# One transformer step on one core: half of the cached attention moved beside an output projection, four adds of squares moved to VectorE

## The chip, the core and the metric

The kernel runs on one core of a Trainium2 chip. The time is the device time of one execution in microseconds (us): the median of three executions of the kernel before is 2620.69 us (2619.88 to 2621.56). A core has engines that run side by side, each in the order of its own instructions: TensorE (PE in the profile, with PEld for its loading of weights), VectorE (DVE), ScalarE (ACT), GpSimd (POOL) and SyncE (SP), which here issues most of the transfers (DMA). An instruction waits on semaphores of the engines or transfers whose results it needs.

## The reference, cut to what matters

One layer of a streaming encoder, for 512 prompt frames and for 8 sequences of 16 new frames each (640 columns in all). The input is normalised and projected, two groups of heads attend, each group's output is normalised by itself, and both together go through one output projection:

```python
def merge_and_ffn(x, oa, ob, norm_grp_a, norm_grp_b, w_out, norm_ffn, w_gate, w_up, w_down):
    o = jnp.concatenate([rmsnorm(oa, norm_grp_a), rmsnorm(ob, norm_grp_b)], axis=-1)
    x = x + o @ w_out
    h = rmsnorm(x, norm_ffn)
    return x + (jax.nn.silu(h @ w_gate) * (h @ w_up)) @ w_down
```

Group A is a chunk-band attention with 16 heads of 64; its 8 sequences also attend to 256 cached keys each ("decode" below). Group B is a grouped-query attention with a window and sinks. Each of oa and ob is 1024 features wide, that is 8 tiles of 128 features x 640 columns.

## The kernel before, in words

All is f32. A product is made of three matmuls on pairs of high and low parts (`mm3`, L207, L208, L209): the high part is a rounded copy (ScalarE, L198, or L202 with a gain), the low part the difference (VectorE, L199 or L203).

The program is emitted as dense matmuls with other work strewn in. The dense work (`dense`) multiplies weights by 640 columns: one k-step is two times three matmuls of 128x320, and after each k-step `tick` adds `rate` to a counter and calls `pump` once for each whole unit. `pump` takes turns over two streams, the prompt heads and decode, and advances one of them to its next `yield`. So `rate` is the pace of the side work against the dense work. `keep_pace` ties each PE instruction of side work behind the dense matmul emitted before it. `drain_queue` pumps until a queue is empty and the work taken from it has ended; `get` pumps where no tile is free. Results of dense work live in two PSUM tiles, named dn, those of side work in tiles named at. The tile names in rows below are the kernel's: S and W are slots of on-chip memory, sm is small numbers, x_d is a tensor in DRAM.

Around the change, in order:

- The input projections run with the heads and decode beside them. `decode_b` and `decode_a(0)` are queued at p == 4 with rate 1.1. `decode_a(g)` does the cached attention of half of group A (heads 8g to 8g + 7): it loads queries, keys and values (sa_d, L655), and then for each of 8 sequences loads cached keys (L677), copies columns (L674), makes scores (mm3 of 128x272), softmax (L697 to L707), loads cached values (L705), transposes the weights (L324), multiplies by the values (128x512), scales (L725), transposes again (L324) and puts the result in its columns (L734). At its end one store (L735) writes the four tiles' columns to oa_d.
- L830 drains decode, so that `decode_a(0)` ends before anything of group B's projection is emitted.
- `group_operands(o_d, gain, ssq, tiles)` loads each tile (L821), splits it with the gain (L202, L203) and adds its squares into the tile ssq (`add_square`: ScalarE squares at L280, the first directly into ssq at L277, and POOL adds at L281). It is called for group B's 8 tiles, then for group A's tiles 0 to 3 (at m == 11) and 4 to 7 (after the loop). All adds of one group go into one tile, one after another.
- `decode_a(1)` is queued.
- Group B's projection: 16 outputs m, each 8 k-steps on the 8 tiles. Behind the first, the sum of squares becomes the factor r_b (`rstd`: L251 sums over partitions, L253 to L258 make the inverse root, L263 spreads it, L268 copies it). Each result is multiplied by r_b (L843), added to x (L844) and stored to x2_d (L845).
- L850 drains all; A's tiles 4 to 7 are made, which need the store L735 of `decode_a(1)`.
- Group A's projection: the same with oa, whose results (L901) are added to what was stored (loads L900, add L902), squared and stored again (L905).

Of the kernel before, what the change touches and what calls it, by code (L numbers as in the profile page):

```python
# [45 lines left out]
def halves(ap):  # L46
    return ap.rearrange("p (a b) -> p a b", a=2)
# [255 lines left out]
def build(nc, tc, io, pools):  # L303
    n = Net(nc, tc, io, pools)
# [15 lines left out]
    def dram(name, shape):  # L320
        return pools["dr"].tile(list(shape), F32, tag=name, name=name)
# [11 lines left out]
    def pair(lst, k=TOK):  # L333
        a, b = n.get(lst), n.get(lst)
        return (a, b), (r(a[:, :k]), r(b[:, :k]))
# [481 lines left out]
    def group_operands(o_d, gain, ssq, tiles):  # L817
        own, out = [], []
        for t in tiles:
            o = n.get("S")  # L820
            dma(out=o, in_=o_d[t])  # L821
            two, hl = pair("S")
            n.split_gain(o, gain[:, t:t + 1], *hl)
            n.add_square(ssq, o, t == 0, "S")
            n.put("S", o)
            own.extend(two)
            out.append(hl)
        return own, out

    n.drain_queue("decode")  # L830
    r_b, ssq = n.get("S"), n.get("S")
    own_b, acts_b = group_operands(ob_d, g_b, ssq, range(8))
    n.add("decode", decode_a(1))
    x2_d, act_d = dram("x2_d", (KT, P, TOK)), dram("act_d", (7, P, NPAIR, 2, HT))
    first_d = dram("first_d", (7, P, 3, HT))
    r_a, ssq_a = n.get("S"), n.get("S")
    for m in range(KT):
        ps = n.dense([(io["w_out_b"][m], 8)], acts_b)
        if m == 0:
            n.rstd(ssq, 1024, r_b)  # L840
        xr, x = n.get("S"), n.get("S")
        dma(out=xr, in_=io["xT"][:, m])
        nc.vector.tensor_tensor(halves(x), ps, halves(r_b), ALU.mult)  # L843
        nc.vector.tensor_tensor(x, x, xr, ALU.add)  # L844
        dma(out=x2_d[m], in_=x)  # L845
        n.put("S", xr, x)
        if m == 11:
            n.drain_queue("heads")
            own_a, acts_a = group_operands(oa_d, g_a, ssq_a, range(4))
    n.drain()  # L850
    n.put("S", r_b, *own_b)
    n.move("D", "S", 10)


    more = group_operands(oa_d, g_a, ssq_a, range(4, 8))
    own_a, acts_a = own_a + more[0], acts_a + more[1]

# [320 lines left out]
    for t in range(STEPS - 2):  # L1178
        run(t)
        if t >= STEPS - 8:  # L1180
            if t == STEPS - 8:
                ssq = n.get("S")
# [143 lines left out]
```

## Time and profile before

| what | value |
|---|---|
| median of three executions | 2620.69 us (2619.88 to 2621.56) |
| the profiled execution | 2621.49 us, span 2619.7 us, mean granted clock of TensorE 0.997 |
| TensorE busy | 2565.2 us, 98% of the span, 17437 matmuls |
| VectorE busy | 2027.7 us, 77% |
| ScalarE busy | 1101.9 us, 42% |
| GpSimd busy | 663.8 us, 25% |
| mean transfer rate | 147 GB/s |

A row of the timeline has the start and duration in us, the engine, the line, the operation, what it writes and reads, the count, and in brackets how long the engine had idled ahead and on whom it waited. A row of the windows has the stretch, its length, the busy time of PE, PEld, VectorE, ScalarE and POOL with counts, the granted clock of TensorE (1.00 is full), the share of the transfer engines and GB/s. Matmuls overlap, so a matmul of 0.31 us may follow another after 0.15.

### The profile page before, as it was taken

How to read it: one execution, taken by the hardware profiler on the slowest of the kernel's cores; microseconds unless marked ns; L12 is line 12 of the kernel's file. 1: busy time of each engine (PE TensorE's matmuls, PEld its weight loads, DVE VectorE, ACT ScalarE, POOL GpSimd, SP SyncE). 2: the span in 40 equal slices, each digit the busy share in tenths (PEclk: the TensorE clock that was granted, in tenths of full speed). 3: DMA queues.
4: the chain of work that ended last, by engine and by line, in shares of the span. 5: the costliest groups of instructions: out<-in, count | busy, mean ns of one | idle time of the engine just before them, and what ended most of it. 6: DMA issues, size and time to landing. Idle time of an engine off the chain costs nothing.

```text
span 2619.7 us, 45100 instructions
## 1 busy us (share of the span) xinstructions
PE 2565.2 (98%) x17437; PEld 2527.9 (96%) x17437; DVE 2027.7 (77%) x3133; ACT 1101.9 (42%) x1797; POOL 663.8 (25%) x573
## 2 busy tenths in 40 slices
PE   8999999999999999999999999999999899999997
PEld 8999998999899999999999999999999899999996
DVE  5775676766866888788888888888888877777797
ACT  5553444444633644443433333433434333333343
POOL 0000000000301203332333333323324433333353
PEclk9999999999999999999999999999999999999998
DMA  5322232444655433443343343343445865666655
GB/s 172 101 69 91 94 102 86 133 124 130 214 188 185 155 131 122 160 162 126 131 142 126 130 144 123 131 146 120 133 147 176 280 189 157 175 175 169 192 156 176
DMA packets 178678, 383.87 MB, mean 147 GB/s; under 512 B 21856, under 2 KB 74080, under 8 KB 178464
## 3 DMA queue, kind: packets, MB, share of 16 engines
q1 hardware_dynamic: 154128, 326.92, 38.8%
q0 software_dynamic: 23184, 52.77, 7.1%
q8 instruction: 137, 2.24, 0.3%
q10 hardware_dynamic: 1152, 1.31, 0.1%
q14 instruction: 77, 0.63, 0.1%
HBM read 299.61 MB, written 80.58 MB: 145 GB/s over the span
## 4 chain that ended last, share of the span: by engine, by line
PE 85%; DVE 8%; DMA 3%; ACT 2%; issue 2%; POOL 0%; SPq 0%; DVEq 0%; ACTq 0%; POOLq 0%
PE dn L209 18%; PE dn L207 18%; PE dn L208 18%; PE at L207 9%; PE at L208 9%; PE at L209 9%; DVE W L199 2%; PE at L324 2%; DMA W<-w_down 1%; PE at L419 1%; DVE S L973 1%; ACT W L198 1%; PE at L215 1%; PE at L214 1%; ACT S L440 0%
## 5 line engine op out<-in xcount | busy, mean ns | idle before, releaser
L207 PE MATMUL dn<-S,W 128*128 128x320 f32 x3694 | 1152.5, 312 | 5.2 <-ACT S L1027 2.7
L209 PE MATMUL dn<-S,W 128*128 128x320 f32 x3694 | 1144.5, 310 | 6.7 <-DVE W L199 6.3
L208 PE MATMUL dn<-S,W 128*128 128x320 f32 x3694 | 1143.3, 310 | 2.0 <-DVE S L203 1.7
L198 ACT ACTIVATE W<-W 128x1024 fp32r<-128x1024 f32 (+2 forms) x632 | 608.2, 963 | 965.9 <-PE dn L208 542.8
L199 DVE TENSOR_TENSOR W<-W,W 128x1024 fp32r<-128x1024 f32 (+2 forms) x632 | 738.7, 1169 | 81.5 <-ACT W L198 77.6
L209 PEld LDWEIGHTS dn<-S,W 128*128 128x128 f32 x3694 | 694.1, 188 | 10.5 <-DVE W L199 10.1
L207 PEld LDWEIGHTS dn<-S,W 128*128 128x128 f32 x3694 | 694.7, 188 | 9.0 <-ACT S L1027 3.0
L208 PEld LDWEIGHTS dn<-S,W 128*128 128x128 f32 x3694 | 694.4, 188 | 4.1 <-DVE S L203 1.9
L209 PE MATMUL at<-S,W 128*128 128x320 f32 x1594 | 493.5, 310 | 4.9 <-DVE W L199 4.8
L207 PE MATMUL at<-S,W 128*128 128x320 f32 x1594 | 492.8, 309 | 0.5 <-ACT W L198 0.5
L208 PE MATMUL at<-S,W 128*128 128x320 f32 x1594 | 492.5, 309 | 0.0
L954 POOL TENSOR_TENSOR W<-W,W 128x1024 f32<-128x1024 f32 (+2 forms) x75 | 158.9, 2118 | 637.5 <-DVE W L199 453.6
L209 PEld LDWEIGHTS at<-S,W 128*128 128x128 f32 x1594 | 299.2, 188 | 7.3 <-DVE W L199 7.3
L207 PEld LDWEIGHTS at<-S,W 128*128 128x128 f32 x1594 | 299.3, 188 | 0.8 <-ACT W L198 0.8
L208 PEld LDWEIGHTS at<-S,W 128*128 128x128 f32 x1594 | 299.3, 188 | 0.0
L973 DVE TENSOR_TENSOR S<-S,dn 128x320 f32<-128x320 f32 x358 | 163.8, 480 | 65.4 <-PE dn L209 65.0
L963 POOL TENSOR_TENSOR W<-W,W 128x1024 f32<-128x1024 f32 (+2 forms) x75 | 163.6, 2181 | 118.9 <-DVE W L199 113.5
L949 DVE TENSOR_TENSOR W<-W,W 128x1024 f32<-128x1024 f32 (+2 forms) x76 | 124.6, 1640 | 62.8 <-DMA W<-w_down 29.5
L973 DVE TENSOR_TENSOR S<-S,at 128x320 f32<-128x320 f32 x262 | 123.3, 480 | 51.4 <-PE at L209 50.5
L980 POOL DMA_DIRECT2D S<-act_d x161 | 88.0, 547 | 178.6 <-PE dn L209 92.0
L951 DVE TENSOR_TENSOR W<-W,W 128x1024 f32<-128x1024 f32 (+2 forms) x76 | 83.4, 1097 | 61.6 <-DMA W<-w_up 31.4
L1044 DVE TENSOR_TENSOR S<-S,half 128x320 fp32r<-128x320 f32 x147 | 120.0, 837 | 1.9
(162 smaller groups left out, 2223.3 us busy)
## 6 DMA issues: line engine op xcount, KB each, us to landing
S<-act_d POOLq DMA_DIRECT2D x161, 320.0 KB, 3.7
W<-w_gate SPq DMA_DIRECT2D x88, 512.0 KB
W<-w_up SPq DMA_DIRECT2D x88, 512.0 KB
W<-w_in SPq DMA_DIRECT2D x66, 512.0 KB
W<-w_down SPq DMA_DIRECT2D x64, 384.0 KB
act_d<-half SPq DMA_DIRECT2D x147, 160.0 KB
act_d<-S SPq DMA_DIRECT2D x147, 160.0 KB
W<-w_down SPq DMA_DIRECT2D x68, 320.0 KB
```

Source lines behind the costliest of these rows:

```text
L198: self.nc.scalar.activation(hi, src, AF.Identity)
L199: self.nc.vector.tensor_tensor(lo, src, f(hi), ALU.subtract)
L207: mm(out, a[0], b[0], start=first, stop=False)
L208: mm(out, a[0], b[1], start=False, stop=False)
L209: mm(out, a[1], b[0], start=False, stop=last)
L949: nc.vector.tensor_tensor(b12[:, w], b12[:, w], b22[:, w], sub)
L951: nc.vector.tensor_tensor(s6[:, w], b11[:, w], b12[:, w], sub)
L954: eng.tensor_tensor(b11[:, w], b22[:, w], s6[:, w], sub)
L963: eng.tensor_tensor(b21[:, w], b21[:, w], s6[:, w], sub)
L973: add = lambda o, a, b: nc.vector.tensor_tensor(o, a, b, ALU.add)
L980: nc.gpsimd.dma_start(out=r(sh(t, 2, HT)), in_=r(act_d[which, :, j]))
L1044: nc.vector.tensor_tensor(r(src), src, hi, ALU.subtract)
```

## The change

The drain at L830 becomes a loop that pumps only until the decode queue is empty, that is, until `decode_a(0)` has been started. What is left of it goes on beside group B's projection, followed by `decode_a(1)`. At m == 11 the same loop makes sure that `decode_a(0)` has ended before A's tiles 0 to 3 are loaded. The rate is 1.22 after `decode_a(1)` is queued, instead of 1.1. In `group_operands`, the squares of tiles with an odd number are added by VectorE instead of POOL. That holds for all calls: tiles 1, 3, 5 and 7 of group B, and those of group A too, eight adds in all. Lines behind the change are two to four further down in the kernel after (L843 is L845, L844 is L846, L845 is L847, L900 is L904, L901 is L905, L905 is L909).

```diff
--- before.py
+++ after.py
@@ -821,16 +821,18 @@
             dma(out=o, in_=o_d[t])
             two, hl = pair("S")
             n.split_gain(o, gain[:, t:t + 1], *hl)
-            n.add_square(ssq, o, t == 0, "S")
+            n.add_square(ssq, o, t == 0, "S", nc.vector if t % 2 else None)
             n.put("S", o)
             own.extend(two)
             out.append(hl)
         return own, out
 
-    n.drain_queue("decode")
+    while n.queues["decode"]:
+        n.pump()
     r_b, ssq = n.get("S"), n.get("S")
     own_b, acts_b = group_operands(ob_d, g_b, ssq, range(8))
     n.add("decode", decode_a(1))
+    n.rate = 1.22
     x2_d, act_d = dram("x2_d", (KT, P, TOK)), dram("act_d", (7, P, NPAIR, 2, HT))
     first_d = dram("first_d", (7, P, 3, HT))
     r_a, ssq_a = n.get("S"), n.get("S")
@@ -846,6 +848,8 @@
         n.put("S", xr, x)
         if m == 11:
             n.drain_queue("heads")
+            while n.queues["decode"]:
+                n.pump()
             own_a, acts_a = group_operands(oa_d, g_a, ssq_a, range(4))
     n.drain()
     n.put("S", r_b, *own_b)
```

In the rows below, what follows the operation is what it writes and, behind the arrow, reads; in brackets stand the engines and transfer queues it waits for.

The first place is PE where the squares of group B are summed over partitions (L251; S_1305 after and S_1369 before is the sum of squares). Before:

```order
4418 L208 MATMUL dn_7978<-S_1383_7768,W_1440_7980 128x320
4419 L207 MATMUL at_7915<-S_1426_7916,S_1409_7836 128x272 [waits PE_49,DVE_49,Activation_49,Pool_49]
4420 L251 MATMUL at_7946<-gains,S_1369_7739 128x1 [waits PE_49]
4421 L251 MATMUL at_7946<-gains,S_1369_7739 128x1 x5
4422 L209 MATMUL dn_7978<-S_1382_7767,W_1441_7981 128x320
```
After:

```order
4352 L207 MATMUL dn_7754<-S_1314_7538,W_1376_7756 128x320
4353 L208 MATMUL dn_7754<-S_1315_7539,W_1376_7756 128x320
4354 L209 MATMUL dn_7754<-S_1314_7538,W_1377_7757 128x320
4355 L251 MATMUL at_7722<-gains,S_1305_7519 128x1 [waits DVE_49]
4356 L251 MATMUL at_7722<-gains,S_1305_7519 128x1 x5
4357 L207 MATMUL dn_7754<-S_1314_7538,W_1376_7756 128x320
```
Before, the sum stood in the first m behind a score product of decode and waited for nothing but PE's own work; now it stands 35 rows behind the transposes (L324) that close a sequence of decode, 27 of them dense, eight of L419, and waits for VectorE.

The second place is VectorE ahead of that, after the change: the adds of tiles 3, 5 and 7 into the sum, each waiting for POOL's add of tile 2, 4 or 6. L421 is a part of the prompt heads' softmax.

```order
1048 L281 TENSOR_TENSOR S_1305_7519<-S_1305_7519,S_1320_7551 128x640 [waits Pool_49]
1049 L421 ISA S_1347_7633,sm_7634<-at_7687,S_1343_7608 128x256 [waits PE_49]
1050 L421 ISA sm_7634 128x1
1051 L421 ISA S_1350_7636,sm_7637<-at_7688,S_1344_7609 128x256 [waits PE_49]
1052 L421 ISA sm_7637 128x1
1053 L281 TENSOR_TENSOR S_1305_7519<-S_1305_7519,S_1328_7569 128x640 [waits Pool_49]
1054 L421 ISA S_1346_7632,sm_7634<-at_7714,S_1343_7608 128x128 [waits PE_49]
1055 L421 ISA sm_7634 128x1
1056 L421 ISA S_1349_7635,sm_7637<-at_7715,S_1344_7609 128x128 [waits PE_49]
1057 L421 ISA sm_7637 128x1
1058 L281 TENSOR_TENSOR S_1305_7519<-S_1305_7519,S_1336_7587 128x640 [waits Pool_49]
```
Before, all seven adds stood on POOL and none of these rows had an add. L734 (two rows) and one L199 stand directly ahead of the first row.

The third place is the passage from group B to group A, where decode's last store (L735) and the loads of A's tiles 4 to 7 (L821) stand in SP's queue. Before:

```order
351 L735 DMA oa_d<-S_1407_7834 128x4x128 [waits DMAHW6_49,DVE_49]
352 L821 DMA S_1728_9573<-oa_d 128x640 [waits DMAHW7_49,DMAHW6_49]
353 L821 DMA S_1732_9582<-oa_d 128x640 [waits DMAHW0_49,Pool_49]
354 L821 DMA S_1736_9591<-oa_d 128x640 [waits DMAHW1_49]
355 L845 DMA x_d<-S_1715_9446 128x640 [waits DMAHW2_49,DVE_49]
356 L821 DMA S_1740_9600<-oa_d 128x640 [waits DMAHW3_49]
357 L219 DMA W_1757_9698<-w_out_a 128x1024 [waits DMAHW4_49,DVE_49]
358 L900 DMA S_1761_9753<-x_d 128x640 [waits DMAHW5_49,DMAHW2_49]
```
After:

```order
353 L847 DMA x_d<-S_1717_9484 128x640 [waits DMAHW0_49,DVE_49]
354 L904 DMA S_1755_9691<-x_d 128x640 [waits DMAHW1_49,PE_49]
355 L904 DMA S_1761_9753<-x_d 128x640 [waits DMAHW2_49,PE_49,Pool_49]
356 L904 DMA S_1777_9846<-x_d 128x640 [waits DMAHW3_49]
357 L735 DMA oa_d<-S_1431_8067 128x4x128 [waits DMAHW4_49,DVE_49]
358 L904 DMA S_1784_9910<-x_d 128x640 [waits DMAHW5_49,PE_49]
359 L821 DMA S_1728_9573<-oa_d 128x640 [waits DMAHW6_49,DMAHW4_49]
360 L821 DMA S_1732_9582<-oa_d 128x640 [waits DMAHW7_49,Pool_49]
```
The store now has three loads of x2_d (L904) directly ahead of it and a fourth between it and the loads of oa_d; before, these followed behind.

On PE at that passage, after the change, the fifth tile of A (S_1729 and S_1730) is used first in row 5364 by dn_9609 (A's first product), 49 rows behind the last transpose of decode (row 5315); before, there were 150 rows between (5209 and 5359).

```order
5360 L209 MATMUL dn_9697<-S_1635_9101,W_1759_9700 128x320 [waits DVE_49]
5361 L207 MATMUL dn_9697<-S_1635_9101,W_1758_9699 128x320
5362 L208 MATMUL dn_9697<-S_1636_9102,W_1758_9699 128x320
5363 L209 MATMUL dn_9697<-S_1635_9101,W_1759_9700 128x320
5364 L207 MATMUL dn_9609<-S_1729_9575,W_1746_9611 128x320 [waits Activation_49]
5365 L207 MATMUL dn_9697<-S_1638_9108,W_1758_9699 128x320
5366 L208 MATMUL dn_9697<-S_1639_9109,W_1758_9699 128x320
5367 L209 MATMUL dn_9697<-S_1638_9108,W_1759_9700 128x320
5368 L207 MATMUL dn_9697<-S_1638_9108,W_1758_9699 128x320
5369 L208 MATMUL dn_9697<-S_1639_9109,W_1758_9699 128x320
5370 L209 MATMUL dn_9697<-S_1638_9108,W_1759_9700 128x320
5371 L208 MATMUL dn_9609<-S_1730_9576,W_1746_9611 128x320 [waits DVE_49]
```
Rows of the second product (dn_9697) now stand between those of the first, and the last tile's low part (S_1742) is waited for in row 5400. Further down, the third product (dn_9790), which needs a PSUM tile that the first has left, now follows close behind L263, of which it needs the result:

```order
5428 L209 MATMUL dn_9697<-S_1741_9602,W_1759_9700 128x320
5429 L263 MATMUL at_9680<-cst,sm_9672 128x128 [waits DVE_49]
5430 L263 MATMUL at_9680<-cst,sm_9672 128x128
5431 L263 MATMUL at_9680<-cst,sm_9672 128x64
5432 L263 MATMUL at_9685<-cst,sm_9672 128x128 x2
5433 L263 MATMUL at_9685<-cst,sm_9672 128x64
5434 L207 MATMUL dn_9697<-S_1741_9602,W_1758_9699 128x320
5435 L208 MATMUL dn_9697<-S_1742_9603,W_1758_9699 128x320
5436 L209 MATMUL dn_9697<-S_1741_9602,W_1759_9700 128x320
5437 L207 MATMUL dn_9790<-S_1635_9101,W_1774_9792 128x320 [waits DVE_49,PE_49]
```
Before, 25 dense rows stood between L263 and the third product; now three do.

## The prediction

> **What bounds the kernel now.** The page comes first: engines, then the chain of waits.
>
> ```profile
> PE 2565.2 (98%) x17437; PEld 2527.9 (96%) x17437; DVE 2027.7 (77%) x3133; ACT 1101.9 (42%) x1797; POOL 663.8 (25%) x573
> PE 85%; DVE 8%; DMA 3%; ACT 2%; issue 2%; POOL 0%; SPq 0%; DVEq 0%; ACTq 0%; POOLq 0%
> ```
>
> TensorE (PE) is busy for 98% of the span. Its count of instructions is not touched by the change, so the change can only win or lose time in which PE stands still or runs at a lower clock. The busy time by stretches, over the decode tail, group B's projection (640 to 815) and one quiet stretch far behind, says how much of that there is. The columns are span, PE, PEld, DVE, ACT and POOL busy time, clock, DMA share and GB/s.
>
> ```profile
> 640.00:660.00 20.00, 18.92 (x122) 17.22 (x121) 14.17 (x30) 11.68 (x22) 2.18 (x4) 1.00 0.74 228
> 660.00:680.00 20.00, 17.58 (x120) 16.11 (x119) 19.74 (x51) 17.12 (x41) 11.14 (x10) 1.00 0.55 170
> 680.00:700.00 20.00, 17.18 (x108) 15.90 (x107) 15.47 (x37) 13.28 (x24) 5.12 (x12) 0.91 0.60 201
> 700.00:720.00 20.00, 19.94 (x132) 18.77 (x130) 12.84 (x29) 6.95 (x13) 2.77 (x10) 1.00 0.75 251
> 720.00:740.00 20.00, 19.65 (x135) 18.90 (x134) 12.86 (x28) 7.41 (x14) 2.13 (x6) 1.00 0.47 153
> 740.00:760.00 20.00, 19.74 (x131) 18.62 (x131) 13.21 (x33) 7.42 (x16) 1.00 (x5) 1.00 0.53 178
> 780.00:800.00 20.00, 18.41 (x124) 17.38 (x123) 14.39 (x27) 9.04 (x16) 6.42 (x6) 1.00 0.65 212
> 688.00:690.00 2.00, 2.00 (x11) 2.00 (x11) 2.00 (x4) 1.97 (x5) 0.61 (x1) 0.55 0.12 40
> 690.00:692.00 2.00, 2.00 (x11) 2.00 (x10) 1.50 (x11) 1.73 (x3) 0.00 (x0) 0.60 0.48 137
> 1000.00:1100.00 100.00, 100.00 (x684) 100.00 (x683) 80.46 (x92) 39.84 (x51) 32.93 (x17) 1.00 0.43 142
> ```
>
> In 640 to 700 PE idles 1.08 + 2.42 + 2.82 = 6.32 us; in 700 to 800 it idles 0.06 + 0.35 + 0.26 + 1.59 = 2.26 us. In 688 to 692 it works at clock 0.55 and 0.60, which costs 2 x 0.45 + 2 x 0.40 = 1.7 us. All that the change can win is therefore about **10.3 us**, 0.39% of the time. The last row gives the price of a dense matmul, 100 / 684 = 0.146 us.
>
> PE's waits between 480 and 900 name the releasers (us in total, times, longest):
>
> ```profile
> PE at L324 <- ACT S L699: 3.5, 6, 1.6
> PE dn L208 <- DVE S L203: 1.7, 1, 1.7
> PE at L324 <- DMA S<-sa_d: 1.5, 1, 1.5
> PE at L207 <- ACT S L198: 1.2, 2, 1.1
> PE at L207 <- DVE S L199: 0.7, 1, 0.7
> ```
>
> These are decode's short serial steps (softmax L699, splits L198 and L199, load of sa_d), unhidden because the drain emits them without dense matmuls around them, and one operand of group B (L203).
>
> **The change part by part.** Rows for the adds of squares, for what stands beside them, and for the two steps of VectorE ahead of the moved ones:
>
> ```profile
> L281 POOL TENSOR_TENSOR S<-S,S x21: 1563/1768/2165, 658.8 to 894.6; 128x640 f32<-128x640 f32 x21
> 929.89 0.82 DVE L281 TENSOR_TENSOR S<-S,S 128x640 f32<-128x640 f32 x1
> 653.90 0.69 DVE L199 TENSOR_TENSOR S<-S,S 128x512 fp32r<-128x512 f32 x1 [1.95 <-ACT S L198]
> 678.88 0.23 DVE L734 COPY S<-at 64x64 f32<-64x64 f32 x1
> 784.65 3.83 POOL L281 TENSOR_TENSOR S<-S,S 128x640 f32<-128x640 f32 x2 [7.99 <-ACT S L280]
> 786.95 1.57 DVE L674 CAST S<-S 64x64 fp32r<-64x64 f32 x1
> 789.51 0.19 DVE L674 CAST S<-S 64x64 fp32r<-64x64 f32 x1
> 790.17 0.62 PE L324 MATMUL at<-cst,S 128*128 128x128 f32 x3 [1.59 <-ACT S L699]
> ```
>
> The helper serves group A too, so eight adds move in all: 8 x 0.82 = 6.6 us more on VectorE, which is 77% busy, and 8 x 1.77 = 14.1 us less on POOL, at 25%. Neither is a gain by itself.
>
> *Start of group B.* The same loads and splits feed the same dense matmuls, now with decode and heads strewn among them. I keep the idle of 640 to 660: 1.1 us (0.5 to 1.5).
>
> *Group B's sum of squares.* All adds go into one tile, so each waits for the one before, now across two engines. By the order, PE stands at L251 27 dense matmuls and eight short L419 products after the transposes that VectorE's L734 waits for: 27 x 0.146 = 3.95 us, plus about 0.8 us estimated for the eight (between the 0.1 of a transpose, four of which take 0.64 to the end below, and the 0.146), 4.75 us. VectorE needs from there 2 x 0.23 + 0.69 + 0.82 = 1.97 us to the third add, and then POOL, VectorE, POOL and VectorE follow in turn: 2 x 1.77 + 2 x 0.82 = 5.2, so 7.15 us. PE waits 2.4 us; with POOL's shortest and longest 2.0 and 3.2. I take 2.6, since VectorE's L421 between its adds can only delay them. Before, L251 waited for PE alone. While VectorE waits for POOL, the L421 behind it wait, and PE's next L419 for their banks. The chain after L251 has a whole m of dense matmuls above it and costs nothing.
>
> *Clock.* A pause may again be followed by a slow stretch. Ahead of the one of before lies this:
>
> ```profile
> 680.00:682.00 2.00, 0.75 (x6) 0.49 (x4) 1.91 (x4) 1.27 (x3) 2.00 (x3) 1.00 1.02 345
> 684.00:686.00 2.00, 0.94 (x7) 0.70 (x6) 1.15 (x4) 1.98 (x5) 0.00 (x0) 1.00 0.97 349
> 2038.00:2046.00 8.00, 5.25 (x37) 5.02 (x36) 7.93 (x10) 3.48 (x8) 6.08 (x7) 1.00 1.12 390
> ```
>
> 2.3 us of idle in these two stretches went before a dip, and 2.75 us at 2038 to 2046 had none within 8 us. So I give a dip after the pause at L251 one half: 0.85 us (0 to 1.7). [...]
>
> *Tail of the heads.* The last prompt products stand closely behind one another, without dense matmuls between; the nearest row is the wait of 1.2 us for L198 above. 0 to 2 us, taken 0.75.
>
> *Decode beside group B.* 1.1 steps of side work per dense step become 1.22, so less dense time lies between a batch's softmax and the transposes that need it. The biggest stall, 1.59 us at 790.17, came from a copy of L674 that took 1.57 instead of 0.19 while POOL added squares, which held L699 back. With half of these adds on VectorE it should go; the short ones double. 2.26 becomes 1.0 (0.7 to 3).
>
> *From B to A.* Decode of A's second half ends later against the dense stream: in the order, 48 dense matmuls lie between its last transpose and the first use of A's fifth tile, where 150 rows did. The way between, in before:
>
> ```profile
> 813.96 0.64 PE L324 MATMUL at<-cst,S 128*128 128x128 f32 x4
> 814.35 0.39 PE L208 MATMUL dn<-S,W 128*128 128x320 f32 x1
> 815.12 0.37 SPq L735 DMA_DIRECT2D oa_d<-S  x1
> 818.56 1.27 SPq L821 DMA_DIRECT2D S<-oa_d  x3
> 821.54 0.83 ACT L202 ACTIVATE S<-S,gains 128x640 fp32r<-128x640 f32 x1 [1.69 <-DMA S<-oa_d]
> 823.82 5.84 DVE L203 SCALAR_TENSOR_TENSOR S<-S,gains,S 128x640 fp32r<-128x640 f32 x3 [0.52 <-ACT S L202]
> 823.15 7.94 POOL L281 TENSOR_TENSOR S<-S,S 128x640 f32<-128x640 f32 x4 [25.57 <-ACT S L280]
> 824.03 6.49 SPq L900 DMA_DIRECT2D S<-x_d  x4
> 844.59 1.23 PE L263 MATMUL at<-cst,sm 128*128 128x128 f32 x10
> 846.32 0.82 DVE L901 TENSOR_TENSOR S<-dn,S 128x640 f32<-128x640 f32 x1 [3.06 <-ACT S L268]
> ```
>
> From 813.96 to the end of L202 at 822.37 are 8.4 us; the cover is 0.39 + 48 x 0.146 = 7.4. That leaves 1.0 us, up to 2.5 if the loads of L904 that now stand ahead of the store delay it; taken 1.6. The other three tiles: the last L203 ended 15.7 us after the transposes; PE needs that operand 36 rows later, at 7.4 + 1.6 + 5.3 = 14.3, so 0 to 1.4 are missing, taken 1.0 since two of the four adds beside it leave POOL. The last add ended 17.1 after; PE is at L251 at about 16: 0 to 1.1, taken 0.3. Last, the third product of A needs the bank that L905 (L901 before) empties after L263 and L268: from the fourth L263 at about 844.95 (844.59 + 3 x 0.12) to the end of L901 at 847.14 are 2.2 us; in the new order three short L263 and three dense matmuls cover about 1.05 of it, where 28 rows did before. 1.15 us. Together **4.05 us** (2.1 to 6.2) where before had none.
>
> **Sum.** 1.1 + 2.6 + 0.85 + 0.75 + 1.0 + 4.05 = 10.35 us against 10.3: a change of 0 (bounds 0.5 + 2.0 + 0 + 0 + 0.7 + 2.1 = 5.3 and 1.5 + 3.2 + 1.7 + 2 + 3 + 6.2 = 17.6, so -5.0 to +7.3). The profiled execution took 2621.49, 0.8 above the median of 2620.69; the sum leaves both where they are: **2621 us**. All behind group A's start I hold at no change, because the engines' order is nearly the old one there.
>
> **The rivals.** *A, faster: both chains are covered.* The stalls of the drain vanish, and PE comes to L251 and to A's fifth tile late enough, because VectorE's earlier work slips less than I have it and the store isn't held. Left are 1.1 + 0.75 + 1.0: 10.3 - 2.9 = 7.4 won, 2613.5 us. For it: in the list of PE's waits above none stands at L251; against: the serial adds are longer than the dense matmuls ahead of L251, by rows.
>
> *B, slower: the store of L735 is held in SP's queue.* Four L900 loads took 6.49 us there at 824.03, with waits for their slots in between. In the new order three such loads stand right ahead of the store and one behind it ahead of L821. If one of these waits as long, the fifth tile comes 5 to 6 us later, and PE waits for all of it: 2621 + 5.5 = 2626.5 us. It decides when the store is issued more than 4 us later after the last transpose than the 1.2 us of before. Against: their slots come from decode tiles used up shortly before.
>
> *C, the reordering hides nothing:* decode steps keep their waits, in new places. PE would idle as before, 2620.7 us; it falls to the same side as the forecast.
>
> **How the numbers follow.** Forecast 0.60, A 0.23, B 0.12, C 0.05. A measurement here tells 0.2% (5.2 us) from no change; so faster 0.23, same 0.65, slower 0.12. The range goes from A's time to just past B's: 2613 to 2627.
>
> **What would show it.** Right: no idle from 660 to 686 as decode's drain had it; PE's wait at L251 on VectorE's L281 of 2 to 3 us; a clock below 1 behind it or not; no 1.57 us copies in L674; about 4 us of waits around L202, L203 and L905 at the start of group A. Wrong: no wait at L251 or at the fifth tile (A), or one wait of over 5 us for oa_d (B).

## The result and the profile after

The change makes the kernel slower: 2629.91 us median of ten (2626.96 to 2637.34) against 2623.43 of before, also of ten (2619.88 to 2626.61); the ratio is **1.0031**, 95% interval 1.0023 to 1.0039. No change was forecast, 2621 us with a range of 2613 to 2627, and the measured time lies above it.

The profiled execution of the change is the slowest of its ten (2637.34 us, span 2635.6), so what follows overstates the loss: 15.9 us by spans, where the medians differ by 6.5. TensorE's busy time and clock by stretches, after the change (span, PE, PEld, VectorE, ScalarE, POOL, clock, DMA share, GB/s):

```profile
640.00:660.00 20.00, 17.77 (x110) 16.67 (x109) 13.09 (x27) 14.16 (x24) 1.11 (x3) 0.91 0.72 238
660.00:680.00 20.00, 16.88 (x102) 15.94 (x101) 14.89 (x38) 7.73 (x12) 5.72 (x5) 0.91 0.46 142
680.00:700.00 20.00, 20.00 (x140) 19.28 (x139) 15.96 (x37) 13.01 (x32) 3.32 (x8) 1.00 0.50 159
700.00:820.00 120.00, 113.83 (x745) 106.62 (x744) 78.83 (x166) 46.06 (x88) 10.71 (x35) 1.00 0.61 193
840.00:860.00 20.00, 16.87 (x101) 16.34 (x99) 8.37 (x13) 9.26 (x14) 3.26 (x2) 0.83 0.49 170
860.00:880.00 20.00, 19.12 (x130) 19.15 (x131) 17.18 (x25) 13.01 (x22) 4.90 (x3) 1.00 0.42 144
```

The drain's idle between 680 and 700 (2.82 us) is gone, as it should be. But 640 to 680 now idles 2.23 + 3.12 = 5.35 us (3.50 before), 700 to 820 idles 6.17 (2.26 before), and 840 to 880 idles 3.13 + 0.88 = 4.01 (none before). Idle grows from 8.58 to 15.53 us. The clock costs 20 x 0.09 + 20 x 0.09 + 20 x 0.17 = 7.0 us where it cost 1.7. That is 6.95 + 5.3 = 12 of the 15.9 us. Of the rest, two slow-clock stretches near 2059 and 2575 (clock 0.50 for 3.4 us, so 1.7 us each) are not in this execution of before; such stretches stand near 2045 and 2580 in kernels of the study that keep decode drained too (e3, e11, e12 and e15, with mean clocks of 0.995 and 0.996 against 0.997 of before), so the change is not what makes them. How much of the median loss of 6.5 us is clock can be estimated from the mean granted clock of all executions: 0.9948 in the ten of the change, 0.9956 to 0.9958 in the later sets of before, so 2 to 2.6 us. PE's waits between 620 and 900 after the change:

```profile
PE at L324 <- ACT S L699: 6.6, 8, 2.1
PE dn L207 <- ACT S L202: 3.0, 1, 3.0
PE at L251 <- DVE S L281: 2.3, 1, 2.3
PE dn L207 <- DVE S L905: 1.0, 1, 1.0
PE dn L208 <- DVE S L203: 0.8, 1, 0.8
PE at L207 <- ACT S L198: 0.8, 1, 0.8
```

Four places carry it. The fences that follow are rows of the timeline. **At the start of group B**, ScalarE and VectorE have its operands' splits and squares around decode's softmax:

```profile
649.46 1.55 ACT L202 ACTIVATE S<-S,gains 128x640 fp32r<-128x640 f32 x2
650.43 0.88 DVE L203 SCALAR_TENSOR_TENSOR S<-S,gains,S 128x640 fp32r<-128x640 f32 x1
650.92 0.72 ACT L280 ACTIVATE S<-S 128x640 f32<-128x640 f32 x1
651.23 0.14 DVE L698 TENSOR_SCALAR sm<-sm 128x1 f32<-128x1 f32 x1
651.54 0.49 ACT L699 ACTIVATE S<-S,sm 128x256 f32<-128x256 f32 x1
652.18 0.62 PE L324 MATMUL at<-cst,S 128*128 128x128 f32 x3 [2.09 <-ACT S L699]
```

L699 comes after three instructions of group B on ScalarE, and PE stands still for 2.09 us in front of the transposes. But L699 could hardly have started sooner: it needs L698, which VectorE finished at 651.37, behind a split of group B (L203). The eleven other kernels of the study that have decode beside group B wait between 0.49 and 1.56 us here, so 2.09 is the largest of all. **At the sum of squares**, VectorE and POOL take turns:

```profile
669.31 0.82 DVE L281 TENSOR_TENSOR S<-S,S 128x640 f32<-128x640 f32 x1
670.21 1.57 POOL L281 TENSOR_TENSOR S<-S,S 128x640 f32<-128x640 f32 x1 [6.81 <-DVE S L281]
671.81 0.82 DVE L281 TENSOR_TENSOR S<-S,S 128x640 f32<-128x640 f32 x1 [0.88 <-POOL S L281]
672.72 1.53 POOL L281 TENSOR_TENSOR S<-S,S 128x640 f32<-128x640 f32 x1 [0.94 <-DVE S L281]
674.28 0.82 DVE L281 TENSOR_TENSOR S<-S,S 128x640 f32<-128x640 f32 x1 [1.23 <-POOL S L281]
675.16 1.05 PE L251 MATMUL at<-gains,S 128*128 128x1 f32 x8 [2.28 <-DVE S L281]
```

POOL had been idle for 6.81 us when VectorE got to the third add; from there the chain takes what its five links take, and L251 follows the last. **Beside group B's projection**, some loads of cached values come late, and ScalarE waits for them in its order with the softmax behind:

```profile
715.54 0.63 ACT L198 ACTIVATE S<-S 128x512 fp32r<-128x512 f32 x1 [3.79 <-DMA S<-cva]
716.08 0.49 ACT L699 ACTIVATE S<-S,sm 128x256 f32<-128x256 f32 x1
716.72 0.62 PE L324 MATMUL at<-cst,S 128*128 128x128 f32 x3 [0.89 <-ACT S L699]
```

Other waits of this stretch have another holder. Here ScalarE stood idle until VectorE gave it L698, and VectorE had a weight split and a sum for group B's result in its order ahead of the softmax (L697):

```profile
731.79 1.22 DVE L199 TENSOR_TENSOR W<-W,W 128x1024 fp32r<-128x1024 f32 x1
732.92 0.82 DVE L846 TENSOR_TENSOR S<-S,S 128x640 f32<-128x640 f32 x1
733.65 0.43 DVE L697 CUSTOM_DVE_ANT_0 S<-at,S 128x272 f32<-128x272 f32 x1
734.62 0.51 ACT L699 ACTIVATE S<-S,sm 128x256 f32<-128x256 f32 x1 [3.38 <-DVE sm L698]
735.28 0.62 PE L324 MATMUL at<-cst,S 128*128 128x128 f32 x3 [0.63 <-ACT S L699]
```

Of the 6.17 us of idle between 700 and 820, three waits stand behind late loads of values (0.89 at 716.72, 0.84 at 719.94, 0.86 at 764.93: 2.6 us), two behind VectorE's work for the dense results (0.63 at 735.28, 0.62 at 811.93: 1.25), and three behind the operands of group A's first tiles on ScalarE and VectorE, in part with dense results between them (0.40 at 780.23, 0.57 at 788.17, 0.85 at 796.46: 1.8), where before had 1.59 at 790.17.

**From B to A**, the way from decode's last transposes to A's fifth tile is longer than before and has less cover:

```profile
833.88 0.60 PE L324 MATMUL at<-cst,S 128*128 128x128 f32 x4
835.00 0.38 SPq L735 DMA_DIRECT2D oa_d<-S  x1
840.70 0.80 SPq L821 DMA_DIRECT2D S<-oa_d  x2
843.66 0.83 ACT L202 ACTIVATE S<-S,gains 128x640 fp32r<-128x640 f32 x1 [5.55 <-DMA S<-oa_d]
844.54 0.90 PE L207 MATMUL dn<-S,W 128*128 128x320 f32 x2 [3.03 <-ACT S L202]
860.88 0.38 PE L207 MATMUL dn<-S,W 128*128 128x320 f32 x1 [0.98 <-DVE S L905]
```

The store went out 1.1 us after the transposes, as before, but the loads could follow only 5.7 us later (3.4 before). This delay is not the order's: e2 and e6, which have the same order in SP's queue (three loads of x2_d some 3.4 to 3.6 us ahead of the store, one behind it), have 3.36 and 3.78 us, and their waits at L202 are 0.65 and 1.04 us. The clock is 0.50 from 843.9 to 850.7, almost seven microseconds; two rows of the windows:

```profile
844.00:846.00 2.00, 1.46 (x5) 1.46 (x6) 0.88 (x1) 1.90 (x4) 0.81 (x1) 0.50 1.00 367
846.00:848.00 2.00, 2.00 (x9) 2.00 (x9) 1.92 (x2) 1.18 (x3) 0.82 (x1) 0.50 0.93 370
```

### The profile page after: what moved, and what is told of

Its sections match the earlier page's. It is cut to its first block, busy times and chain, and to the rows that moved or that the text cites. A ratio compares the mean times of both kernels' runs of the same rounds, so it can differ in the third digit from the quotient of the medians.

```text
span 2635.6 us, 45097 instructions
## 1 busy us (share of the span) xinstructions
PE 2573.9 (98%) x17437; PEld 2535.8 (96%) x17437; DVE 2026.7 (77%) x3141; ACT 1102.4 (42%) x1797; POOL 647.1 (25%) x565
## 4 chain that ended last, share of the span: by engine, by line
PE 83%; DVE 8%; DMA 4%; ACT 2%; issue 2%; POOL 0%; SPq 0%; DVEq 0%; ACTq 0%; POOLq 0%
PE dn L207 18%; PE dn L209 18%; PE dn L208 17%; PE at L207 9%; PE at L209 9%; PE at L208 9%; DVE W L199 2%; PE at L324 2%; PE at L419 1%; DMA W<-w_down 1%; DVE S L977 1%; DMA W<-w_in 1%; DVE S L199 1%; ACT W L198 1%; PE at L215 1%
## 5 line engine op out<-in xcount | busy, mean ns | idle before, releaser
L198 ACT ACTIVATE W<-W 128x1024 fp32r<-128x1024 f32 (+2 forms) x632 | 608.3, 963 | 956.2 <-PE dn L208 533.5
L199 DVE TENSOR_TENSOR W<-W,W 128x1024 fp32r<-128x1024 f32 (+2 forms) x632 | 739.1, 1170 | 81.0 <-ACT W L198 77.4
```

The lines of the kernel that those rows point to most:

```text
L198: self.nc.scalar.activation(hi, src, AF.Identity)
L199: self.nc.vector.tensor_tensor(lo, src, f(hi), ALU.subtract)
```

## The experiments

Ratios are to the kernel before, measured beside it on the same chip. The change consists of three parts: the **place** of decode's first half, the **pace** and the **squares**.

### The three parts, each undone and each alone

Pace undone (e1), in the change:

```diff
-    n.rate = 1.22
```

> The change with its pace alone undone (1.1 again, as before, beside group B). Theory 1, the way from B to A is too short: by the order the fifth tile of A is then used 2.5 us of PE work behind decode's last transposes (7.0 in the change), while the way takes 8.4 to 11; PE waits some 5 us more there, and saves 1 to 2 us of the short waits for L699: 3 to 4 us slower than the change, ratio to before 1.004 to 1.005. Theory 2, the higher pace is the cost (softmax too close to its transposes): most of the 4.4 us of waits for L699 go, ratio 1.001 to 1.002.

1.0056 (1.0043 to 1.0069), slower than the change. PE's waits in its profile:

```profile
PE at L324 <- ACT S L699: 7.2, 7, 2.6
PE dn L207 <- ACT S L202: 4.0, 1, 4.0
PE dn L207 <- DVE S L904: 1.8, 1, 1.8
```

The wait at A's fifth tile (L202) and at the PSUM bank (L904 here) grow from 4.0 to 5.8 us, less than the 5 us more that were expected, and the waits at L699 don't shrink. Theory 2, that the pace is the cost, falls; the pace gives some of the loss back.

Squares undone (e2), in the change:

```diff
-            n.add_square(ssq, o, t == 0, "S", nc.vector if t % 2 else None)
+            n.add_square(ssq, o, t == 0, "S")
```

> The change with all seven squares of group B and four of A's eight... all of A's too, added by POOL again; pace and place of decode stay. Theory 3, the chain of adds waits in VectorE's queue behind heads and decode: POOL alone ends it some 3 to 4 us earlier, PE's wait of 2.3 us at L251 goes and the slow clock behind it (1.7 us) may: 2 to 4 us faster than the change, ratio 1.0015 to 1.0025. Its rival, POOL is the slow part of the chain: six adds of 1.57 to 2.1 us on POOL end later, the wait grows by 1 to 3 us: ratio 1.0035 to 1.0045.

1.0045 (1.0033 to 1.0058), against 1.0031 (1.0023 to 1.0039): not faster. The chain on POOL did end earlier, but another wait stands beside it in the timeline:

```profile
662.65 7.14 POOL L281 TENSOR_TENSOR S<-S,S 128x640 f32<-128x640 f32 x4
671.70 0.52 PE L419 MATMUL at<-W,W 128*128 128x128 f32 x3 [2.13 <-DVE S L734]
672.88 2.51 PE L251 MATMUL at<-gains,S 128*128 128x1 f32 x12 [0.67 <-DVE sm L421]
```

POOL's last add ends at 669.8, and L251 waits 0.67 us, but PE already waited 2.13 us a microsecond earlier for L734, which stood in VectorE's order behind a late split; its first half (L198, at 669.83) had stood on ScalarE until that last add of POOL. Theory 3 had the chain right and the gain wrong.

Place undone (e3), with pace and squares of the change:

```diff
-    while n.queues["decode"]:
-        n.pump()
+    n.drain_queue("decode")
     r_b, ssq = n.get("S"), n.get("S")
```

> The drain of decode ahead of group B is back; pace 1.22 and the adds on VectorE stay. Theory 1: the cost hangs on the place of decode's first half; the fifth tile of A has 30.8 us of PE work as cover (21.8 before), no wait there; with 1 to 2 us more at L699 for the pace and L251 as before: ratio 0.999 to 1.001. Theory 2, the pace is the cost: 1.002 or more.

1.0009 (1.0000 to 1.0018). Most of the loss goes with the place of decode's first half.

A higher pace (e4):

```diff
-    n.rate = 1.22
+    n.rate = 1.35
```

> The change with a pace of 1.35 instead of 1.22. Theory 1: decode's second half ends earlier, 16.7 us of PE work cover the way to A's fifth tile, the waits of 3.0 and 1.0 us and the slow clock behind them (3.4) go, 1 us more at L699: 4 to 6 us faster than the change, ratio 1.0005 to 1.0015. Theory 2: more waits at L699, 2 to 4 us slower than the change, ratio 1.004 to 1.005.

1.0035 (1.0024 to 1.0047). The waits at the passage did go, as theory 1 had it: the stretch from 820 to 900 is busy for all of its 80 us. But the time did not follow, since 700 to 820 now idles 10.9 us, by the windows of e4:

```profile
700.00:820.00 120.00, 109.09 (x690) 102.27 (x690) 77.27 (x163) 45.47 (x87) 12.12 (x36) 0.96 0.55 180
```

The new waits in its timeline:

```profile
709.42 0.63 ACT L198 ACTIVATE S<-S 128x512 fp32r<-128x512 f32 x1 [3.83 <-DMA S<-cka]
716.26 0.69 PE L324 MATMUL at<-cst,S 128*128 128x128 f32 x2 [4.35 <-ACT S L699]
```

A late load of keys holds ScalarE for 3.83 us, and PE then waits 4.35 us for L699. Neither theory had both halves.

The last three combinations, run later: place alone (e13), squares alone (e15) and pace alone (e16), each with the other two undone by the diffs above (e13: those of e1 and e2; e15: e1 and e3; e16: e2 and e3).

> Only decode's first half goes on beside group B; pace 1.1, all squares on POOL. If the place of decode is the cost: as e1 and e2, ratio 1.005 to 1.007, with waits at L202 and the bank at the passage to A of 5 to 6 us together (A's fifth tile has 2.5 us of cover by the order), 3 to 6 us at L699. If place, pace and squares must come together to cost: 1.002 or less.

> The kernel before with only the odd squares on VectorE, in one sum as in the change. The chain is covered there (the order has PE at L251 some 13 us of work later than the change): ratio 0.9995 to 1.0005; if handing to and fro between the engines costs everywhere, a wait of 1 to 2 us at L251 and 1.001.

> The kernel before with only the pace of 1.22 beside group B. Decode's second half ends earlier, which nobody waits for; softmax and transposes lie closer together: 0.5 to 2 us more at L699: ratio 1.0002 to 1.0008. If the pace is harmless: 1.000.

1.0059 (1.0047 to 1.0072), 0.9999 (0.9990 to 1.0008) and 1.0006 (0.9997 to 1.0015). With these, all eight combinations are measured:

| place of decode's first half | pace 1.1, squares on POOL | pace 1.1, squares shared | pace 1.22, squares on POOL | pace 1.22, squares shared |
|---|---|---|---|---|
| drained ahead of B | 1 (before) | 0.9999 | 1.0006 | 1.0009 |
| beside B | 1.0059 | 1.0056 | 1.0045 | 1.0031 (the change) |

Decode beside group B costs 0.2 to 0.6% in each column. The pace and the squares cost little or nothing where decode is drained (1.0009 together, with an interval from 1.0000); beside B they give back about half of the loss. The pace does so clearly with the squares shared (1.0056 to 1.0031); what sharing the squares does there can't be told from zero (1.0059 to 1.0056 at pace 1.1, and 1.0045 to 1.0031 at 1.22, with intervals that overlap).

### Why the loads are late

Loads on POOL's queue (e5), in `decode_a` of the change:

```diff
-                dma(out=sh(raws[hf], 2, CA), in_=io["cka"][b, g, hf])
+                nc.gpsimd.dma_start(out=sh(raws[hf], 2, CA), in_=io["cka"][b, g, hf])
...
-                dma(out=raws[j][:, :512], in_=io["cva"][b, g, j])
+                nc.gpsimd.dma_start(out=raws[j][:, :512], in_=io["cva"][b, g, j])
```

> The change with decode's loads of cached keys and values (L677 and L705) issued by POOL instead of SP; nothing else. Theory 4, loads that stand late in SP's queue (behind the stores and weight loads of group B) hold ScalarE, and with it VectorE and the softmax: ScalarE's waits for cka and cva (8.5 and 23.8 us between 640 and 860 in the change) fall to a third, PE's waits for L699 between 700 and 820 from 4.4 to 2 us or less: 2 to 4 us faster than the change, ratio to before 1.0015 to 1.0025. Its rival, the pace (too little dense work between a softmax and its transposes): the waits of ScalarE fall, those of PE stay at 4 us or more: ratio 1.003.

1.0092 (1.0076 to 1.0108), far slower. Theory 4 falls: on a queue that has no stores or weights in it, the loads still waited for others. The answer of the trace on line L705, on whom POOL waited ahead of these loads in the whole program:

```profile
L705 POOL DMA_DIRECT2D S<-cva x32: 536/536/559, 485.5 to 820.3; - x32
  PE at L209: 20.2, 7
  DVE S L281: 11.1, 1
```

These two are the longest of ten. In the kernel a load waits for the last use of the tile that it is to fill. POOL's copies for the scores (L686) stand behind the waiting loads (POOL idled for 4.94 us ahead of a load of values at 708.15, and a copy follows at 708.69), which makes e5 more than a change of queue.

Values loaded earlier (e8), directly behind the keys:

```diff
                 dma(out=sh(raws[hf], 2, CA), in_=io["cka"][b, g, hf])
+            vraws = n.get("S"), n.get("S")
+            for j in range(2):
+                dma(out=vraws[j][:, :512], in_=io["cva"][b, g, j])
             yield
...
-            raws = n.get("S"), n.get("S")
-            for j in range(2):
-                dma(out=raws[j][:, :512], in_=io["cva"][b, g, j])
+            raws = vraws
```

> The change with the loads of cached values issued together with those of the keys, some steps earlier, on SP; it holds two tiles more for that time. Theory 4: ScalarE's wait of 23.8 us for cva falls below 8, PE's waits for L699 fall by 1 to 2 us: ratio 1.002 to 1.0025. The rival: 1.003 or, since the tiles run out earlier and work is pumped ahead, more.

1.0018 (1.0009 to 1.0027): faster than the change, as theory 4 and theory 6 (the tiles, stated with the next run) both allow; ScalarE's wait for cva (23.8 us in the change) fell to almost nothing, but that for cka (8.5) rose, and PE's waits at L699 between 700 and 820 did not fall (6.0 us against 4.5).

Values in other tiles (e9): the two loads fill one W tile, which is 1024 wide, instead of two S tiles.

```diff
-            raws = n.get("S"), n.get("S")
+            vraw = n.get("W")
             for j in range(2):
-                dma(out=raws[j][:, :512], in_=io["cva"][b, g, j])
+                dma(out=vraw[:, 512 * j:512 * j + 512], in_=io["cva"][b, g, j])
...
-                n.split(raws[j][:, :512], *vd)
-                n.put("S", raws[j])
+                n.split(vraw[:, 512 * j:512 * j + 512], *vd)
+                if j:
+                    n.put("W", vraw)
```

> The change with each pair of cached-value loads going into one W slot (1024 wide, idle here) instead of two S slots; queue and pace as in the change. Theory 6: the loads are late because their S slots are still held, 16 of them by group B's operands while both halves of decode run beside them, and not because of SP's queue. ScalarE's wait of 23.8 us for cva (640 to 860) falls below 10, the waits of PE for L699 and L198 between 700 and 820 (5.3 us) to 3 or less: 1.5 to 3 us faster than the change, ratio 1.0015 to 1.0025. Rival, the pace: PE's waits stay at 5 us, ratio 1.003.

1.0008 (0.9999 to 1.0016): most of the loss is gone, with two S tiles less for each sequence and nothing else changed by hand. That tiles held these loads is shown: the last of them goes out at 714.0 us, where it went out at 811.5 in the change, and ScalarE's wait for cva is gone. But its wait for the keys (cka) rose from 8.5 to 21.1 us, and PE's waits at L699 between 700 and 820 stayed at 4.6 us, against what theory 6 had. By the windows, first of e9, then of e6 (two sums, the next section), which leaves the loads in S tiles:

```profile
640.00:700.00 60.00, 56.91 (x376) 54.07 (x375) 45.42 (x105) 35.24 (x70) 8.42 (x13) 0.97 0.66 216
820.00:900.00 80.00, 77.30 (x524) 75.87 (x523) 58.68 (x87) 41.97 (x67) 16.04 (x9) 1.00 0.50 174
```

```profile
640.00:700.00 60.00, 57.60 (x378) 54.56 (x377) 47.43 (x106) 35.72 (x71) 10.59 (x14) 0.97 0.63 204
700.00:820.00 120.00, 116.12 (x766) 109.50 (x765) 77.95 (x166) 45.80 (x90) 10.65 (x36) 1.00 0.60 192
820.00:900.00 80.00, 76.23 (x517) 74.88 (x516) 58.66 (x85) 41.72 (x65) 15.83 (x9) 1.00 0.49 167
```

In e9, 640 to 700 idles 3.1 us instead of 5.35, 700 to 820 4.83 instead of 6.17, 820 to 900 2.7 instead of 4.0, and the passage has no slow clock (1.00 from 820 to 900). But e6 has 2.4, 3.9 and 3.8 us and no slow clock at the passage either (1.00), without that edit, and what both are compared with is the slowest execution of the change. So the times show that tiles (S), of which group B keeps 16 for its operands, are part of what decode lacks beside it; where in the trace that gain falls is not shown. Nor does ScalarE's waiting measure the loss: in before it waits 15.9 us for cka and 10.3 for cva between 640 and 860, and PE's waits at L699 between 700 and 820 are 2.1 us. The rival that is left, a greater distance between a softmax and its transposes, was not tried; it would hold more of the 62 S tiles at once.

### The chain of adds, and the parts mended together

Two sums (e6): the change, with even tiles summed by POOL in one tile and odd ones by VectorE in another:

```diff
-            n.add_square(ssq, o, t == 0, "S", nc.vector if t % 2 else None)
+            n.add_square(other if t % 2 else ssq, o, t < 2, "S", nc.vector if t % 2 else None)
+            if t == 7:
+                nc.vector.tensor_tensor(ssq, ssq, other, ALU.add)
...
```

> The change with the squares of even tiles summed in one tile by POOL and those of odd tiles in another by VectorE, and one add of the two by VectorE at the end: one add more for each group, but no handing to and fro. Theory 5, the alternating chain is what PE waits for at L251: its wait of 2.3 us falls below 0.5 and the slow clock behind it goes: 2 to 4 us faster than the change, ratio 1.0015 to 1.0025. Its rival, VectorE's queue itself is late there (heads and decode ahead of the adds): the wait stays at 1.5 us or more, ratio 1.003.

1.0012 (1.0003 to 1.0021), as theory 5 had it and a little better. The wait at L251 fell from 2.3 to 0.3 us. The slow clock behind it, which theory 5 had go too, stayed: from 672.5 to 676 dense matmuls start 0.27 us apart, where it was 0.15 just before, and the clock of 660 to 680 is 0.91.

Two sums with the diffs of e5 and e4 (e7), two sums with that of e9 (e10), and e10 with a third pace (e14):

```diff
-    n.rate = 1.22
+    n.rate = 1.30
```

> Both edits together and a pace of 1.35, which took the waits at the passage from B to A away. By theories 4 and 5 with it, 1 to 2 us are left at 650, 1 at L251 and 3 at L699 where before had 10.3: ratio 0.998 to 1.0. By the rivals (pace, VectorE's queue) the waits for L699 stay at 9 us: 1.003.

> The two-sum squares of the run before and the loads of cached values in W slots, at a pace of 1.22. By theories 5 and 6 both gains add: ratio 0.9995 to 1.0005, with about 1 us at 650, 2 at L699 and 4 at the passage to A left. If the pace decides: 1.001 as with the two sums alone.

> e10 at a pace of 1.30. In the order decode's last transposes come 3.4 us of PE work earlier against group A than in e10, so the waits there (4 us with the bank's 1.9) fall below 2; if the pace then costs nothing at L699 (5 us or less as in e10): ratio 0.9995 to 1.0005. If the pace costs as much as the passage saves: 1.001 as e10.

1.0046 (1.0034 to 1.0059), 1.0010 (1.0001 to 1.0019) and 1.0011 (1.0002 to 1.0019). e7 fails with POOL's loads. In e10 the two gains don't add: what is left is the passage and L699. At 1.30 the idle of 820 to 900 falls from 3.2 to 0.8 us, and that of 700 to 820 grows from 4.9 to 6.1, with two slow stretches between 640 and 900 (clock 0.99 in 700 to 820 and 0.92 in 840 to 860) where e10 has one (0.99 in 700 to 820).

Both decode halves beside group B thus came to 1.0008 at best (e9), with paces of 1.22, 1.30 and 1.35 tried along with the mends.

The diff of e6 in the kernel before, with decode drained and the pace 1.1 (e11), and that of e9 with it (e12):

> The kernel before (decode drained ahead of group B, pace 1.1) with the squares in two sums, even tiles on POOL, odd on VectorE. If POOL's adds beside VectorE's splits cost the waits at 664 (1.7 us) and 788 (1.6) of before, 1 to 3 us of them go: ratio 0.999 to 0.9995. If not (the chain was covered anyway and VectorE has more to do): 1.000 to 1.0005.

> The same with the loads of cached values in W slots. ScalarE's waits for cva (10.3 us in before) fall below 5; by theory 6 the remaining short waits at L699 shrink by 0.5 to 1 us: ratio 0.9985 to 0.9995. If slots were no bound before (one half of decode alone beside group B): as e11.

**0.9988** (0.9979 to 0.9997) and 0.9997 (0.9988 to 1.0006). e11 is the only kernel of the study that beats both: 2619.88 us median beside 2622.48. Its windows:

```profile
640.00:700.00 60.00, 55.44 (x360) 50.39 (x360) 52.10 (x123) 43.34 (x87) 12.83 (x24) 1.00 0.71 229
700.00:820.00 120.00, 118.10 (x784) 112.89 (x783) 75.60 (x156) 42.76 (x80) 10.34 (x26) 1.00 0.59 189
```

640 to 700 idles 4.56 us where before idled 6.32, the clock stays at 1.00, and the waits of 1.7 us at L203 and 1.6 us at 790 are gone. That would fit POOL's adds beside VectorE as their cause, but e12, with the same two sums, still waits 1.47 us at L203 (666.59) and 1.04 at L699 (791.94). So the cause is open; the gain is small and its interval ends close to 1. The W tiles show no gain here (e12), where decode is drained.

## Why the prediction was wrong

Its working gave 10.35 us of lost time for the change; the profiled execution has 15.53 + 7.0 = 22.5. That execution is the slowest of ten, so each term is also held against other kernels of the study with decode beside group B. Term by term:

- *Start of group B*, 1.1 predicted: 2.23 idle in 640 to 660, but 0.9 to 1.7 in e1, e2, e4, e6, e8, e9 and e13. The size was fair; the wait was another. The term was taken over from before, where decode's softmax cost 0.35 us here (at 650.21); now L698 and L699 stand between splits and squares of group B on VectorE and ScalarE, which the working did not look for.
- *Sum of squares*, 2.6: **2.28**, and 2.2 to 2.6 in e1, e4, e5 and e9 (1.3 in e8). Right, by the chain that was given, and confirmed by e6, which takes it away. Not seen was that another wait stands beside it: with all adds on POOL (e2) the time is no better.
- *Clock*, 0.85: **7.0**. The size failed, and the term was given to one place only, at a chance of one half. A clock of 0.50 followed the pauses at 652 (2.09 us) and 675 (2.28), and set in 0.6 us before the end of that at 844 (3.03). Behind a wait of 1.3 us or more at L251 all six kernels that have one (the change, e1, e4, e5, e8 and e9) show a slow stretch; the clock of 660 to 680 is 0.91 in the change and in e9, and the mean clock of the six profiled executions 0.992 to 0.996, where before had 0.997.
- *Tail of the heads*, 0.75: 0; its place has the 0.84 for an operand (L203).
- *Decode beside group B*, 1.0 (0.7 to 3): **6.17**, and 3.9 to 7.0 in the other kernels at pace 1.22 with the loads on SP (e2, e6, e8, e9 and e10). This is the step that failed worst. It held the waits at before's level but for the pace and one slowed copy. The copy did go (no L674 takes over 0.2 us in the change), and yet 1.8 us stand behind group A's first operands in the place of its 1.59; 1.25 us stand behind VectorE's work for the dense results; and 2.6 us behind loads of values, which e9 shows to be late for want of tiles. No run takes these waits away together: e9 ends the third kind and still idles 4.83 us there, so what each of them would give back alone stays open.
- *From B to A*, 4.05: **4.01** (3.13 and 0.88 by the windows). The sum is luck in this execution: 3.03 us of it are one wait for the fifth tile, whose loads came 2.3 us later than in before, which e2, e6 and e9 don't have. These three idle 3.23, 3.77 and 2.70 us at the passage in the several waits that were forecast, at L202, L203 and the bank; so the mechanism held, and the size roughly.

Rival B falls by its own sign: the store went out 1.1 us after the transposes, where more than 4 us over the 1.2 of before would have spoken for it, and PE's wait there was 3.03 us, not over 5. Rivals A and C fall: two chains were not covered, and the drain's waits did go. The sum's bounds (up to +7.3 us) held the median loss of 6.5, but the range was cut at 2627 from the chance given to B. The half rate (0.50) behind the pauses of 2.1 and 2.3 us lasted 3.4 us (652.7 to 656.1 and 676.6 to 680.0), as long as that of before (688.2 to 691.6), and twice as long, 6.8 us, at 844 (843.9 to 850.7).

## What to carry to other kernels

Moving a serial piece of work beside dense work traded its old waits for new ones here: the idle of 2.82 us between 680 and 700 went, and that between 700 and 820 grew from 2.26 to 6.17. Some loads slipped because the dense work's operands held tiles (the last load of values went out at 811.5 us, and at 714.0 in e9), and VectorE and ScalarE, each in its order, had work for the dense results (1.25 us of waits) and operands (1.8 us) ahead of the softmax that PE waited for. Before such a move, count the free tiles, and on each engine list what will stand ahead of the step that PE waits for. A sum that was added by two engines in turn did better here as two sums joined once (1.0031 to 1.0012).

## What was not expected of the hardware

In the change, pauses of TensorE of 2.09, 2.28 and 3.03 us came with half rate (clock 0.50) for 3.4, 3.4 and 6.8 us, which by the clock costs 1.7, 1.7 and 3.4 us more. That was not always so: in e9 a pause of 2.2 us (L251) had a slow stretch within 5 us behind it (0.91 in 660 to 680) and one of 2.7 us (L324, near 714) had none (1.00 in 700 to 820). Nor did a slow stretch always have such a pause ahead of it: in e6 one begins at 672.5 (0.91 in 660 to 680) where the waits of the ten microseconds before are 0.3 to 0.4 us each. What sets it off is open. The profiled execution of the change has five such stretches, one of double length (from 652.7, 676.6, 843.9, 2059.0 and 2574.4), beside the one at the program's end (0.50 from 2622, and in before from 2606), and took 2637.34 us; the ten spread over 10.4 us, those of before over 6.7. A transfer that another waits for (oa_d, stored and loaded again) was followed by its loads 3.4 us after its issue in before, 3.55 in e9 and 5.70 in the change. Why is open: three loads of L904 went out some 3.4 us ahead of the store in the change, and as far ahead in e9, and e2 and e6 with the same order have 3.36 and 3.78.
